# Half of the memory is turned within the half-wide chunk of the first net; turned rows lie in two tiles of weight blocks

## The chip, the cores and the metric

The kernel runs on one core of a Trainium2 chip. The core has a matrix engine (PE, whose weight loads the profile lists apart as PEld), a vector engine (DVE), a scalar engine (ACT), a general engine (POOL) and a queue that issues transfers (SP). Each engine runs its own instructions strictly in the order that the program gives it and waits on semaphores for the others. The metric is the device time of one execution in microseconds (us); before the change it is 1070.46 us, the median of three runs.

## What is computed

The reference is a decoder of two layers over 256 tokens of width 1024 with a memory of 256 rows. In each layer stand a gated net, a mixer, a cross attention into the memory and a second gated net, each with a residual sum and a layer norm. Cut to what matters here:

```python
h = x
for l in range(DEPTH):
    h = layer_norm(ALPHA * h + 0.5 * swiglu(h, ffn1_gate[l], ffn1_up[l], ffn1_down[l]), ...)
    ...                                  # mixer: z = h @ w_in[l], convolution, recurrence, pooling
    h = layer_norm(ALPHA * h + mix, ...)
    h = layer_norm(ALPHA * h + cross_attn(h, mem, ca_q[l], ca_k[l], ca_v[l], ca_o[l]), ...)
    h = layer_norm(ALPHA * h + 0.5 * swiglu(h, ffn2_gate[l], ffn2_up[l], ffn2_down[l]), ...)

def cross_attn(x, mem, wq, wk, wv, wo):
    q, k, v = x @ wq, mem @ wk, mem @ wv     # in four heads
    ...
def swiglu(x, w_gate, w_up, w_down):
    return (jax.nn.silu(x @ w_gate) * (x @ w_up)) @ w_down
```

The hidden width of a net is 2816. The memory `mem` is the same in both layers.

## The kernel before

**Products in two parts.** Every fp32 operand of a large product is split into a high part, rounded for PE's fast format (`whi`, `ah`, the first half of `xT` and `mT`), and a remainder (`wlo`, `al`, the second half). The helper `split` does it with two instructions: a cast on ACT (line 75) and a subtraction on DVE (line 76). A product is then three matmuls: high by high, remainder by high, high by remainder (line 129 issues them all). Weights come by transfers on SP into `raw` tiles of 1024 columns (6 buffers), and the parts into `whi` and `wlo` (8 buffers each), so a cast into `whi` waits until PE has left the tile eight before it.

**The net.** `ffn` runs over chunks of 512 hidden columns; 2816 is five such chunks, 0 to 4, and a last one, chunk 5, of 256 (`last_hidden`). Chunks 2 and 4 (`sevens`) take their products from seven block products instead of eight (`by_seven`), with weight blocks in tiles named `spare0`, `spare1`, `spare2`, `lng`, `lnb` and `raw`. The activations of a chunk are gated on DVE (line 690 for the sevens, line 706 for the last chunk), brought into the order of the second product (`turn`: four transfers and DVE transposes, line 472), and split into `ah` and `al`. The second product of a chunk is run later by `both` into four banks `dn`; the last products, of chunks 4 and 5, stand in `tail`, called from `finish`. For each row tile of 128 tokens and each half of 512 columns, `finish` adds the residual on DVE as soon as that bank is done (line 353), takes the mean and on ACT the squares (line 366), and scales in two steps (lines 374 and 379). PE then transposes the row tile of `h` (line 196) for the next stage: row tile 0 within the tail of row tile 1, row tile 1 within the next stage.

**The memory.** The keys of layer 0 are the stage behind the first net, and they read `mT`, the memory with its width on the partitions and split into two parts. `load_memory` fetches the rows in blocks of 32 into `early_memory` in the middle of the net (POOL's queue, at 100 us), and returns `later`, called `turn_memory` at its use. It turns the blocks of 32 by 32 on DVE (line 220) into `turned`, a tile of tag `up`, of which there is one buffer, and splits `turned` into `mT0` and then `mT1`. `mT1` takes the place of `early_memory`, so its parts are written when all rows have been turned. Before the change this is called once chunk 5 has been recorded, and its instructions on DVE are held behind the last weight remainder recorded until then (`tc.issue_after(lows[-1].ins)`; `lows` lists the subtractions of all splits).

**What sets the order.** Except for a few stretches written by hand, a scheduler orders each engine's instructions when the program is built: by the order in which the code records them, as far as their inputs, free buffers and the edges of `issue_after` allow. An edge holds only instructions of the engine of the instruction that it names. The place where a call stands in the code therefore moves its own instructions and others around them.

## Time and profile before

| what | before |
|---|---|
| median of three runs | 1070.46 us (1069.86 to 1070.7) |
| the profiled execution's own time | 1068.35 us |
| its span, from the first instruction to the last | 1066.6 us |
| granted clock of the matrix engine, mean of the span | 0.998 |
| stretch 129 to 158 us: DVE busy | 23.84 of 29 us |
| stretch 158 to 169 us: DVE busy | 10.89 of 11 us |

The tables of the profile that follow in the prediction are read like this. A timeline row begins with the start in us from the span's start and the time that the row takes, then engine, line, operation, output<-inputs and the form; x3 behind it means three instructions in a row. A bracket gives the idle time of the engine ahead of the row and what ended it. A row of the chain of waits has start, length and what the end of the program was waiting for at that time. A row of waits reads: who waited <- for whom: us in total, times, longest. A PE row's length is from a matmul's start to its end; the next one starts some 0.216 us behind it (512 columns). Tile names are those of the code, without numbers.

### The profile page before, as it was taken

To read this page: it belongs to the slowest core of one execution; us is meant where nothing else is said; L and a number is where in the kernel's file an instruction comes from. 1 tells how busy PE (TensorE), PEld (TensorE's weight loads), DVE (VectorE), ACT (ScalarE), POOL (GpSimd) and SP (SyncE) were. 2 spreads that over 40 slices of the span, in tenths; PEclk is the share of its full clock that TensorE was granted. 3 is DMA by queue.
4 is the path that set the end of the run, shared out by engine and by line. 5 is a ranking of instruction groups with operands and counts; after the bars stand their busy time and mean duration, and the time that the engine had idled before them with its cause. 6 is when DMAs were issued, how large, how long until landed. Compare 5 with 4: busy or idle time off the path is not lost.

```text
span 1066.6 us, 16319 instructions
## 1 busy us (share of the span) xinstructions
PE 1054.6 (99%) x5954; PEld 935.1 (88%) x5954; DVE 915.1 (86%) x1225; ACT 658.8 (62%) x903; POOL 87.2 (8%) x119
## 2 busy tenths in 40 slices
PE   9999999999999999999999999999999999999997
PEld 7888888989899888888888888888998998888886
DVE  6998888989988789897798988689899788899885
ACT  7675765677557557656575757466774655665660
POOL 8001001000000001010001000010000000000000
PEclk9999999999999999999999999999999999999999
DMA  9999983754575589979588978756636675899861
GB/s 364 292 304 297 263 280 116 262 176 159 196 277 172 169 281 238 357 173 293 172 293 221 334 230 258 261 178 217 201 117 222 241 241 165 241 291 304 215 213 40
DMA packets 138897, 248.70 MB, mean 233 GB/s; under 512 B 9472, under 2 KB 48672, under 8 KB 138816
## 3 DMA queue, kind: packets, MB, share of 16 engines
q1 hardware_dynamic: 129024, 228.49, 64.2%
q0 software_dynamic: 9216, 17.98, 9.7%
q10 hardware_dynamic: 576, 1.18, 0.3%
q8 instruction: 47, 0.77, 0.3%
q14 instruction: 34, 0.28, 0.1%
HBM read 232.93 MB, written 1.05 MB: 219 GB/s over the span
## 4 chain that ended last, share of the span: by engine, by line
PE 97%; DVE 2%; DMA 0%; issue 0%; ACT 0%; DVEq 0%; ACTq 0%
PE acc L129 65%; PE dn L129 29%; PE acc L196 1%; DMA h<-in_x_dram 0%; PE dn L990 0%; DVE turned L220 0%; DVE wlo L76 0%; PE dn L1064 0%; DVE mT L76 0%; DVE h L379 0%; PE dn L1063 0%; PE dn L1052 0%; PE acc L1132 0%; DVE h L374 0%; PE dn L1015 0%
## 5 line engine op out<-in xcount | busy, mean ns | idle before, releaser
L76 DVE TENSOR_TENSOR wlo<-raw,whi 128x1024 fp32r<-128x1024 f32 (+1 forms) x444 | 525.9, 1214 | 60.5 <-ACT whi L75 46.1
L75 ACT CAST whi<-raw 128x1024 fp32r<-128x1024 f32 (+1 forms) x444 | 449.9, 1043 | 199.2 <-PE dn L129 63.8
L129 PE MATMUL acc<-whi,xT 128*128 128x512 f32 x992 | 300.7, 379 | 0.0
L129 PEld LDWEIGHTS acc<-whi,xT 128*128 128x128 f32 x992 | 187.5, 189 | 26.5
L129 PE MATMUL acc<-wlo,xT 128*128 128x512 f32 x496 | 188.0, 379 | 0.0
L129 PE MATMUL acc<-xT,whi 128*128 128x512 f32 x576 | 141.0, 381 | 0.2
L129 PE MATMUL dn<-whi,ah 128*128 128x512 f32 x346 | 131.5, 380 | 0.0
L129 PE MATMUL dn<-wlo,ah 128*128 128x512 f32 x346 | 131.1, 379 | 0.0
L129 PE MATMUL dn<-whi,al 128*128 128x512 f32 x346 | 131.1, 379 | 0.0
L129 PEld LDWEIGHTS acc<-xT,whi 128*128 128x128 f32 x576 | 104.1, 190 | 12.5 <-ACT whi L75 0.8
L129 PEld LDWEIGHTS acc<-wlo,xT 128*128 128x128 f32 x496 | 93.8, 189 | 13.2
L129 PE MATMUL dn<-whi,xT 128*128 128x512 f32 x288 | 87.8, 381 | 0.0
L129 PEld LDWEIGHTS acc<-xT,wlo 128*128 128x128 f32 x576 | 75.5, 191 | 3.9
L129 PE MATMUL acc<-xT,wlo 128*128 128x256 f32 x576 | 75.9, 275 | 0.0
L129 PEld LDWEIGHTS dn<-whi,al 128*128 128x128 f32 x346 | 65.4, 189 | 9.3
L129 PEld LDWEIGHTS dn<-wlo,ah 128*128 128x128 f32 x346 | 65.4, 189 | 9.2
L129 PEld LDWEIGHTS dn<-whi,ah 128*128 128x128 f32 x346 | 65.4, 189 | 9.1
L129 PEld LDWEIGHTS dn<-whi,xT 128*128 128x128 f32 x288 | 54.4, 189 | 7.6 <-DVE xT L76 0.2
L129 PE MATMUL dn<-wlo,xT 128*128 128x512 f32 x144 | 54.6, 379 | 0.0
L371 POOL TENSOR_TENSOR rs<-rs,nhalf 128x1 f32<-128x1 f32 x16 | 15.0, 935 | 457.1 <-DVE rs L367 326.4
L129 PE MATMUL acc<-whi,kTh 128*128 128x512 f32 x128 | 48.5, 379 | 0.0
L129 PE MATMUL acc<-wlo,kTh 128*128 128x512 f32 x128 | 48.5, 379 | 0.0
(240 smaller groups left out, 1286.0 us busy)
## 6 DMA issues: line engine op xcount, KB each, us to landing
raw<-in_ffn_up_dram SPq DMA_DIRECT2D x88, 512.0 KB, 5.7
raw<-in_ffn_down_dram SPq DMA_DIRECT2D x88, 512.0 KB, 5.9
raw<-in_ffn_gate_dram SPq DMA_DIRECT2D x84, 512.0 KB, 5.4
raw<-in_w_in_dram SPq DMA_DIRECT2D x48, 512.0 KB, 4.7
dealt<-sg SPq DMA_DIRECT2D x80, 128.0 KB, 5.0
raw<-in_ffn_up_dram POOLq DMA_DIRECT2D x16, 512.0 KB, 7.2
raw<-in_ffn_gate_dram POOLq DMA_DIRECT2D x16, 512.0 KB, 9.2
raw<-in_ca_k_dram SPq DMA_DIRECT2D x16, 512.0 KB, 4.8
```

The costliest lines, as they stand in the source:

```text
L75: nc.scalar.copy(hi, src)
L76: lows.append(nc.vector.tensor_tensor(lo, src, hi.bitcast(F32), op=ALU.subtract))
L129: nc.tensor.matmul(o, w, x, start=start, stop=stop, skip_group_check=more)
L196: nc.tensor.transpose(pt[:, k, :], src[:, (4 * j + k) * P : (4 * j + k + 1) * P], unit)
L371: nc.gpsimd.tensor_tensor(rs, rs, nhalf[:, 0:1], op=ALU.pow)
```

## The change

`later` now takes two numbers, the half of the memory `n` and the pair of blocks `k`, and does a quarter of the work at each call. `turned` lies in the tiles `spare2` (first half) and `spare0` (second half), no longer in the tag `up`, which the last chunk itself uses for its `up` product. `last_hidden` calls it: the two quarters of the first half around the load of the gate weights, one of them held on DVE behind the gating product of chunk 4 (`passed[-1]`), the other behind the last remainder of the gate weights; the two quarters of the second half at its end, as before behind the chunk's own remainders.

```diff
-        def later():
-            for n in range(2):
-                turned = mp.tile([P, NT, CHUNK], F32, tag="up", name="turned", bufs=1)
-                for k in range(2):
-                    nc.vector.transpose(
-                        turned[:, k, :].rearrange("p (k b j) -> p k b j", k=2, j=32),
-                        m[:, 4 * n + 2 * k : 4 * n + 2 * k + 2],
-                    )
+        turned = {}
+
+        def later(n, k):
+            if not k:
+                o = mp.tile([P, DM], F32, tag=("spare2", "spare0")[n], name="turned", bufs=1)
+                turned[n] = o.rearrange("p (k t) -> p k t", t=SEQ)
                 mT.tiles[n] = cst.tile([P, 4, 2, SEQ], F32R, tag=f"mT{n}", name=f"mT{n}")
-                for k in range(2):
-                    d = slice(4 * n + 2 * k, 4 * n + 2 * k + 2)
-                    split(mT[:, d, 0, :], mT[:, d, 1, :], turned[:, k, :].rearrange("p (k t) -> p k t", k=2))
+            o = turned[n][:, k : k + 2]
+            nc.vector.transpose(o.rearrange("p k (b j) -> p k b j", j=32), m[:, 4 * n + k : 4 * n + k + 2])
+            d = slice(4 * n + k, 4 * n + k + 2)
+            split(mT[:, d, 0, :], mT[:, d, 1, :], o)
...
-                    nc.vector.tensor_tensor(s, s, ef, op=ALU.mult)
+                    passed.append(nc.vector.tensor_tensor(s, s, ef, op=ALU.mult))
...
                 for m, o in ((gate, s), (up, r)):
+                    if turn and m is gate:
+                        with tc.issue_after(passed[-1].ins):
+                            turn(0, 0)
                     w = load(m, 0, NK, c0, 2 * P)
+                    if turn and m is gate:
+                        with tc.issue_after(lows[-1].ins):
+                            turn(0, 2)
...
+                if turn:
+                    with tc.issue_after(lows[-1].ins):
+                        turn(1, 0)
+                        turn(1, 2)
                 return ah, al
...
-                    acts.append(hidden(c0) if ncol == CHUNK else last_hidden(c0))
+                    acts.append(hidden(c0) if ncol == CHUNK else last_hidden(c0, turn_memory))
...
-                if c == 5 and early is not None:
-                    with tc.issue_after(lows[-1].ins):
-                        turn_memory()
```

The orders of PE, SP and POOL are the same but for line numbers. Three places of DVE and ACT matter. The first is DVE at the end of chunk 4, from the second difference of its halves (line 643, which was 644) to the last quarter of the first half; `wlo` are weight remainders. Before, and then now, where the rows begin behind the first of these differences and three weight remainders:

```order
L644 TENSOR_TENSOR halves<-acc,halves 128x512
L76 TENSOR_TENSOR wlo<-raw,whi 128x1024 x4
L644 TENSOR_TENSOR halves<-acc,halves 128x512
L76 TENSOR_TENSOR wlo<-raw,whi 128x1024 x2
L644 TENSOR_TENSOR halves<-acc,halves 128x512
L76 TENSOR_TENSOR wlo<-raw,whi 128x1024 x2
L690 TENSOR_TENSOR sg<-sg,halves 128x1024
L76 TENSOR_TENSOR wlo<-raw,whi 128x1024 x4
```

```order
L224 STREAM_TRANSPOSE turned<-early_91 128x512
L76 TENSOR_TENSOR wlo<-raw,whi 128x1024
L643 TENSOR_TENSOR halves<-acc,halves 128x512
L76 TENSOR_TENSOR mT_1344<-turned,mT_1344 128x2x256
L76 TENSOR_TENSOR wlo<-raw,whi 128x1024
L643 TENSOR_TENSOR halves<-acc,halves 128x512
L76 TENSOR_TENSOR wlo<-raw,whi 128x1024 x3
L689 TENSOR_TENSOR sg<-sg,halves 128x1024
L224 STREAM_TRANSPOSE turned<-early_91 128x512
L76 TENSOR_TENSOR wlo<-raw,whi 128x1024 x2
L76 TENSOR_TENSOR mT_1344<-turned,mT_1344 128x2x256
```

Two transposes and two remainders of the memory have come in, the first pair ahead of the fourth split of a row, the second behind the gating product of chunk 4.

The second place is DVE from the gating product of chunk 5 (line 706, now 711) to the residual sums of row tile 0 (line 353, now 352). Before, and then now:

```order
L706 TENSOR_TENSOR sg<-up,sg 128x512
L76 TENSOR_TENSOR al<-sg,ah 128x256 x2
L220 STREAM_TRANSPOSE turned<-early_91 128x512 x2
L76 TENSOR_TENSOR wlo<-raw,whi 128x1024
L76 TENSOR_TENSOR mT_1456<-turned,mT_1456 128x2x256 x2
L76 TENSOR_TENSOR wlo<-raw,whi 128x1024
L220 STREAM_TRANSPOSE turned<-early_91 128x512 x2
L353 TENSOR_SCALAR h_72,st<-h_72,dn 128x512
L76 TENSOR_TENSOR mT_1464<-turned,mT_1464 128x2x256 x2
L353 TENSOR_SCALAR h_72,st<-h_72,dn 128x512
```

```order
L711 TENSOR_TENSOR sg<-up,sg 128x512
L76 TENSOR_TENSOR wlo<-raw,whi 128x1024
L76 TENSOR_TENSOR al<-sg,ah 128x256 x2
L224 STREAM_TRANSPOSE turned<-early_91 128x512 x2
L76 TENSOR_TENSOR wlo<-raw,whi 128x1024
L76 TENSOR_TENSOR mT_1458<-turned,mT_1458 128x2x256 x2
L352 TENSOR_SCALAR h_72,st<-h_72,dn 128x512 x2
```

Two transposes and two remainders are gone from behind the chunk, the two residual sums follow each other, and one weight remainder, of the key weights, has moved ahead of `al`.

The third is ACT at the end of chunk 5, from the casts of the `up` product's weights on. Before, and then now:

```order
L149 COPY up<-acc 128x256 x2
L75 COPY whi<-raw 128x1024
L75 COPY ah<-sg 128x256 x2
L75 COPY whi<-raw 128x1024
L75 COPY mT_1456<-turned 128x2x256
L75 COPY whi<-raw 128x1024
L75 COPY mT_1456<-turned 128x2x256
L75 COPY mT_1464<-turned 128x2x256 x2
```

```order
L149 COPY up<-acc 128x256 x2
L75 COPY whi<-raw 128x1024 x2
L75 COPY ah<-sg 128x256 x2
L75 COPY whi<-raw 128x1024
L75 COPY mT_1458<-turned 128x2x256 x2
```

One more weight cast stands ahead of `ah`; two of the four casts into `mT` have left this place and stand among the weight casts of the first place.

More of the change, by code (lines that the diff above doesn't have):

```diff
@@ L689, in left, with last_hidden @@
                     put(e, o[3], ALU.add, e)
-                    nc.vector.tensor_tensor(s, s, ef, op=ALU.mult)
+                    passed.append(nc.vector.tensor_tensor(s, s, ef, op=ALU.mult))
                     return turn(s)
                 return left
-            def last_hidden(c0):
+            def last_hidden(c0, turn=None):
                 ah, al = act_tiles()
@@ L720, in ffn @@
             sevens = (2, 4)
+            passed, turn_memory = [], None
             bx = []
```

## The prediction

> **What bounds the kernel now.** I read the page first, then the waits of the matmul engine, then the chain of waits around the memory's turning, then the timelines of single engines.

> ```profile
> PE 1054.6 (99%) x5954; PEld 935.1 (88%) x5954; DVE 915.1 (86%) x1225; ACT 658.8 (62%) x903; POOL 87.2 (8%) x119
> ...
> PE 97%; DVE 2%; DMA 0%; issue 0%; ACT 0%; DVEq 0%; ACTq 0%
> ```

> PE works almost without a break and is 97% of the chain. A change on DVE and ACT can matter only where PE stands still. The waits of PE, over the whole span (us in total, times, longest):

> ```profile
> PE acc L196 <- DVE h L379: 1.9, 1, 1.9
> PE dn L493 <- DVE kTh L488: 1.5, 1, 1.5
> PE acc L512 <- DMA h<-in_x_dram: 0.7, 2, 0.5
> ```

> The last two are the start of the program. The first is the one stall behind it, and it happens once: PE is to transpose row tile 0 of `h` behind the first net of layer 0, and the normalized tile is late. PE's timeline there, and at the same place of layer 1, where no memory is turned:

> ```profile
> 170.79 0.38 PE L129 MATMUL dn<-whi,al 128*128 128x512 f32 x1
> 173.10 1.29 PE L196 MATMUL acc<-idn,h 128*128 128x128 f32 x8 [1.93 <-DVE h L379]
> ...
> 174.44 0.38 PE L129 MATMUL dn<-wlo,ah 128*128 128x512 f32 x1
> ```

> ```profile
> 698.32 0.38 PE L129 MATMUL dn<-whi,al 128*128 128x512 f32 x1
> 698.54 1.04 PE L196 MATMUL acc<-idn,h 128*128 128x128 f32 x8
> ...
> 699.63 0.38 PE L129 MATMUL dn<-wlo,ah 128*128 128x512 f32 x1
> ```

> From the last product ahead of the transposes to the second behind them: 174.44 - 170.79 = 3.65 us in layer 0, 699.63 - 698.32 = 1.31 in layer 1. The same instructions cost 2.34 us more where the memory is turned. That is the prize, and all of it.

> Why the tile is late, from the chain:

> ```profile
> 157.49 0.88 DVE al L76 x2
> ...
> 159.05 2.15 DVE turned L220 x2
> ...
> 164.64 2.04 DVE turned L220 x2
> ...
> 167.35 1.29 DVE mT L76 x2
> 168.65 0.62 DVE h L353 x2
> ...
> 172.20 0.76 DVE h L379
> ```

> The four transposes of the memory and their four remainders stand on DVE between the chunk's last split (`al`) and the residual sums of line 353; the second residual sum begins at 168.57 in DVE's timeline, shown below beside layer 1's, which waits for PE alone.

> **The change, part by part.** The work itself stays the same:

> ```profile
> L220 DVE STREAM_TRANSPOSE turned<-early x4: 1132/1144/1184, 159.1 to 165.5; 128x512 f32<-128x512 f32 x4
> L75 ACT CAST mT<-turned x4: 613/616/618, 160.2 to 167.2; 128x512 fp32r<-128x512 f32 x4
> L76 DVE TENSOR_TENSOR mT<-turned,mT x4: 685/714/741, 162.2 to 168.0; 128x512 fp32r<-128x512 f32 x4
> ```

> Four transposes, four casts, four subtractions before and after; nothing on PE, SP or POOL moves. Half of them, 2 x 1.144 + 2 x 0.714 = 3.72 us of DVE and 2 x 0.616 = 1.23 us of ACT, go ahead.

> *Where the first half goes.* One transpose now stands ahead of the third weight split of this stretch, the other behind the gating product of chunk 4. DVE and PE there:

> ```profile
> 129.43 3.82 DVE L76 TENSOR_TENSOR wlo<-raw,whi 128x1024 fp32r<-128x1024 f32 x3 [1.24 <-ACT whi L75]
> ...
> 142.05 1.23 DVE L76 TENSOR_TENSOR wlo<-raw,whi 128x1024 fp32r<-128x1024 f32 x1 [0.57 <-ACT whi L75]
> 143.74 1.23 DVE L76 TENSOR_TENSOR wlo<-raw,whi 128x1024 fp32r<-128x1024 f32 x1 [0.46 <-ACT whi L75]
> 147.29 1.23 DVE L76 TENSOR_TENSOR wlo<-raw,whi 128x1024 fp32r<-128x1024 f32 x1 [2.33 <-PE acc L129]
> ...
> 143.97 1.05 PE L129 MATMUL acc<-xT,wlo 128*128 128x256 f32 x8
> ```

> The third split of the first row ends at 133.25 and PE first reads it at 143.97: 10.7 us in hand against one transpose (1.14) and the cast wait on ACT behind it. DVE's idle time behind the moved rows (0.57 + 0.46 + 2.33 = 3.36 us) nearly holds the 3.72, so I count nothing. If that cover is gone, the lateness reaches the next part, where it has a price.

> *What stands ahead of the chunk's own split now.* With `raw` and `whi` free, the scheduler put the first split of the key weights between the product `sg` and `al`, on ACT and DVE both. Before:

> ```profile
> 156.54 0.38 PE L129 MATMUL dn<-whi,al 128*128 128x512 f32 x1
> 156.58 1.70 ACT L75 CAST ah<-sg 128x256 fp32r<-128x256 f32 x2 [2.18 <-DVE sg L706]
> 157.49 1.67 DVE L76 TENSOR_TENSOR al<-sg,ah 128x256 fp32r<-128x256 f32 x2 [1.00 <-ACT ah L75]
> 160.86 0.19 PEld L129 LDWEIGHTS dn<-whi,al 128*128 128x128 f32 x1
> 161.51 0.19 PEld L129 LDWEIGHTS dn<-whi,al 128*128 128x128 f32 x1
> 160.74 1.04 ACT L75 CAST whi<-raw 128x1024 fp32r<-128x1024 f32 x1
> 161.06 1.24 DVE L76 TENSOR_TENSOR wlo<-raw,whi 128x1024 fp32r<-128x1024 f32 x1
> ```

> The cast is the one at 160.74, the split the one at 161.06. There are 8 `whi` buffers; this cast takes the one that PE leaves with the matmul of 156.54 (the last product of that weight tile), so it can start near 156.54 + 0.38 = 156.9 and ends near 158.0 (1.04). `ah` then starts at 158.0, not 156.58. On DVE the weight split runs from 158.0 to 159.15 (the next instruction starts 1.1 us behind it), and `al` from 159.15 to 160.8. PE loads the first `al` at 160.86, the second at 161.51; ready at about 160.0 and 160.8, where before it was 158.35 and 159.16. The margins shrink from 2.5 and 2.35 us to about 0.85 and 0.7. No stall, but this is the thinnest place of the change.

> *What is left behind the chunk.* Two transposes, one weight split, two remainders. The old timeline has the same five from 159.05 to the split below, 163.36 - 159.05 = 4.31 us; `al` itself held DVE from 157.49 to 159.05, 1.56. So 159.15 + 1.56 + 4.31 = 165.0, and the first residual sum, 0.7 us, ends at 165.7. The second cannot start before PE has finished its bank:

> ```profile
> 163.36 1.28 DVE L76 TENSOR_TENSOR wlo<-raw,whi 128x1024 fp32r<-128x1024 f32 x1
> ...
> 165.61 0.38 PE L129 MATMUL dn<-whi,al 128*128 128x512 f32 x1
> 168.57 0.68 DVE L353 SCALAR_TENSOR_TENSOR h<-h,dn 128x512 f32<-128x512 f32 x1
> 693.56 0.69 DVE L353 SCALAR_TENSOR_TENSOR h<-h,dn 128x512 f32<-128x512 f32 x1 [3.19 <-PE dn L129]
> ```

> That is 165.61 + 0.38 = 166.0, with DVE 0.3 us early; layer 1's sum waits for PE in the same way, and starts 0.04 behind it. So the chain starts 168.57 - 166.03 = 2.54 us sooner, the first half of `h` is done at 172.20 + 0.76 - 2.54 = 170.4, and PE comes to the transposes at 170.79 + 0.22 = 171.0. The pause closes with about 0.6 us over. What is late next: nothing at this place; row tile 1 and the keys follow PE as they do in layer 1.

> *The sum.* Profiled execution 1068.35 us (span 1066.6) - 2.34 = 1066.0. It lies 2.11 below the median of the runs, 1070.46; the same step on the median gives 1068.1. Bounds of the step: 1.93, if only the pause of PE's row closes, and 2.54, the whole advance of the chain. I take 2.34 because layer 1 shows the same instructions without the pause.

> The pause has another size on the weight loads:

> ```profile
> 173.07 0.42 PEld L196 LDWEIGHTS acc<-idn,h 128*128 128x128 f32 x4 [2.30 <-issue]
> 173.73 0.42 PEld L196 LDWEIGHTS acc<-idn,h 128*128 128x128 f32 x4 [0.24 <-PE acc L196]
> ```

> [...]

> **The rivals.** *A smaller pause takes the old one's place.* DVE has 0.3 us over ahead of the second sum and the chain 0.6 behind it. If the row through `al` comes 1.5 us later than worked out (one more weight split of 1.14 and a cast wait), about 0.7 us of stall comes back: 1068.8. For it: both margins are thin and ACT and DVE now wait for each other twice more. Against it: the dates above already hold the split and the cast. At 3 us the gain would be down to nothing.

> *The gain is hidden anyway.* PE runs 2.3 us earlier into the mixer and waits there for transposed rows or weights. Against it: PE's list of waits has no second entry, and layer 1 arrives there without the pause and pays nothing for it. Price: all of it, 1070.4.

> *Slower.* The split through `al` becomes PE's bound. None of the 3.72 us is absorbed ahead of 147.29, since that idle time ends by PE and not by DVE, and all of it comes out on the chunk's chain. `al` is then ready at 160.0 + 3.7 = 163.7 against 160.86: a new stall of 2.9 in the place of 2.34, so 1070.46 + 2.84 - 2.34 = 1071.0. It decides from a lateness of 0.85 + 2.34 = 3.2 us. For it: DVE is 86% busy. Against it: 3.36 us of idle time and more than 10 us in hand at the split that was displaced.

> *The change doesn't do what it says.* The order of DVE shows two of four transposes moved, so I give this no chance of its own.

> **How the numbers follow.** Forecast 0.72, smaller pause 0.15, hidden 0.07, slower 0.06. The predicted time is 1068.1. The forecast's own range: 1070.46 - 2.54 - 0.6 = 1067.3 (0.6 is how far the lowest run lies under the median) to 1070.46 - 1.93 + 0.24 = 1068.8. With most of the smaller pause taken in: 1067.2 to 1069.5. What a measurement of this kernel can tell from no change is about 0.2%, 2.14 us, which is 1068.32: my forecast lies 0.2 us beyond it, so I give three quarters of its 0.72 to faster, 0.54, and one hundredth from the rest for a step larger than worked out: faster 0.55. Slower by over 0.2% begins at 1072.6, beyond the 1071.0 of the slower rival; I let two thirds of that rival's chance run past it, since a chain of late waits between two engines need not stop at the sum of the moved work: 0.04. Same takes the rest, 0.41.

> **What would show it.** In the changed profile: PE's wait for the `h` of line 379 (378 in the changed kernel) is gone from its list; the transposes of `h` follow the product ahead of them within 0.25 us and take 1.04, not 1.29; the second residual sum carries idle time released by PE; the whole-tile splits ahead of chunk 5 run later and PE does not wait for one. The smaller-pause rival would show as a wait of PE for `al`, or again for `h`, under 1 us; the slower one as a PE wait for `al` above 2 us. The prediction is wrong if PE's busy share and its list of waits stay as they are, or if a new wait appears between 129 and 162 us.

## The result, and the profile after

| what | before | after |
|---|---|---|
| median, seven runs of each | 1070.46 us (1068.75 to 1070.83) | 1066.25 us (1065.96 to 1067.75) |
| ratio over all runs, 95% interval | | 0.9966 [0.9954, 0.9978] |
| the profiled execution's own time | 1068.35 us | 1066.03 us |
| its span | 1066.6 us | 1064.3 us |

By the ratio over all runs, which is not the quotient of the medians, the change makes the kernel faster by 0.34% (0.22 to 0.46). Between the medians it is 4.21 us, which is 0.39%, and between the means of the same runs 1070.20 - 1066.55 = 3.6 us. The forecast was 1068.1, with a range that ended at 1067.2: the time lies below it. Yet between the two profiled executions the step is 1068.35 - 1066.03 = 2.32 us, where the sum had 2.34. Both figures are real, and the rest of this document is about the difference between them.

The page of the changed kernel, busy times and the chain by engine, and then PE's complete list of waits:

```profile
PE 1054.4 (99%) x5954; PEld 935.3 (88%) x5954; DVE 915.1 (86%) x1225; ACT 658.3 (62%) x903; POOL 87.4 (8%) x119
...
PE 99%; DMA 0%; DVE 0%; issue 0%; ACTq 0%; DVEq 0%
```

```profile
PE dn L492 <- DVE kTh L487: 1.5, 1, 1.5
PE acc L511 <- DMA h<-in_x_dram: 0.5, 1, 0.5
```

Busy times are the same to 0.5 us. What is gone is the wait for `h`: no entry of PE's list lies behind the start of the program, and DVE's share of the chain has fallen from 2% to nothing. PE's timeline at the transposes of row tile 0 of `h`:

```profile
170.85 0.38 PE L129 MATMUL dn<-whi,al 128*128 128x512 f32 x1
171.07 1.04 PE L196 MATMUL acc<-idn,h 128*128 128x128 f32 x8
171.86 0.46 PE L129 MATMUL dn<-whi,ah 128*128 128x512 f32 x1
172.16 0.38 PE L129 MATMUL dn<-wlo,ah 128*128 128x512 f32 x1
```

From the product ahead of the transposes to the second behind them it is 172.16 - 170.85 = 1.31 us, which is what layer 1 takes, against 3.65 before. DVE and ACT on the way there:

```profile
131.93 1.11 DVE L224 STREAM_TRANSPOSE turned<-early 128x512 f32<-128x512 f32 x1
...
141.54 1.13 DVE L224 STREAM_TRANSPOSE turned<-early 128x512 f32<-128x512 f32 x1
...
147.35 1.23 DVE L76 TENSOR_TENSOR wlo<-raw,whi 128x1024 fp32r<-128x1024 f32 x1 [0.69 <-ACT whi L75]
149.09 1.23 DVE L76 TENSOR_TENSOR wlo<-raw,whi 128x1024 fp32r<-128x1024 f32 x1 [0.52 <-ACT whi L75]
...
157.36 0.69 DVE L711 TENSOR_TENSOR sg<-up,sg 128x512 f32<-128x512 f32 x1
158.11 1.22 DVE L76 TENSOR_TENSOR wlo<-raw,whi 128x1024 fp32r<-128x1024 f32 x1
159.25 1.59 DVE L76 TENSOR_TENSOR al<-sg,ah 128x256 fp32r<-128x256 f32 x2
160.76 2.11 DVE L224 STREAM_TRANSPOSE turned<-early 128x512 f32<-128x512 f32 x2
...
165.10 0.68 DVE L352 SCALAR_TENSOR_TENSOR h<-h,dn 128x512 f32<-128x512 f32 x1
...
166.09 0.69 DVE L352 SCALAR_TENSOR_TENSOR h<-h,dn 128x512 f32<-128x512 f32 x1 [0.30 <-PE dn L129]
```

```profile
157.02 1.05 ACT L75 CAST whi<-raw 128x1024 fp32r<-128x1024 f32 x1 [1.15 <-PE dn L129]
158.14 1.68 ACT L75 CAST ah<-sg 128x256 fp32r<-128x256 f32 x2
```

The idle time of 2.33 us that ended by PE before 147.29 is gone; the split that stood behind it starts at 147.35, so up to there the first half of the memory was paid out of idle time. Behind it DVE does fall back. The split at 149.09 stood behind the sums `sg` of line 150 before (at 150.42) and now stands ahead of the transposes of line 472 (now 471). This move is not among the places listed under the change. DVE waits there for a cast, and the gating product of chunk 5 (line 706, now 711, the row at 157.36 above) starts 1.56 us later than before, where it was:

```profile
155.80 0.68 DVE L706 TENSOR_TENSOR sg<-up,sg 128x512 f32<-128x512 f32 x1
```

It costs nothing, because `ah` cannot start before the weight cast ahead of it has ended, at 157.02 + 1.05 = 158.07, and the late product ends at 157.36 + 0.69 = 158.05. The two meet within 0.02 us. The weight cast starts when PE leaves the `whi` tile, `ah` follows at 158.14, `al` stands on DVE from 159.25 to 160.76, and the second residual sum, at 166.09, has 0.30 us of idle time ended by PE: DVE is early there and PE late, as in layer 1.

### The profile page after: what moved, and what is told of

It reads as the page before. It is cut to its first block, busy times and chain, and to the rows that moved or that the text cites. A ratio compares the mean times of both kernels' runs of the same rounds, so it can differ in the third digit from the quotient of the medians.

```text
span 1064.3 us, 16318 instructions
## 1 busy us (share of the span) xinstructions
PE 1054.4 (99%) x5954; PEld 935.3 (88%) x5954; DVE 915.1 (86%) x1225; ACT 658.3 (62%) x903; POOL 87.4 (8%) x119
## 3 DMA queue, kind: packets, MB, share of 16 engines
HBM read 232.93 MB, written 1.05 MB: 220 GB/s over the span
## 4 chain that ended last, share of the span: by engine, by line
PE 99%; DMA 0%; DVE 0%; issue 0%; ACTq 0%; DVEq 0%
PE acc L129 65%; PE dn L129 31%; PE acc L196 1%; DMA h<-in_x_dram 0%; PE dn L997 0%; PE dn L1071 0%; PE dn L1070 0%; PE dn L1059 0%; PE acc L1139 0%; PE dn L1022 0%; DVE h L378 0%; PE acc L511 0%; DVE h L373 0%; DVE st L358 0%; DVE h L346 0%
## 5 line engine op out<-in xcount | busy, mean ns | idle before, releaser
L76 DVE TENSOR_TENSOR wlo<-raw,whi 128x1024 fp32r<-128x1024 f32 (+1 forms) x444 | 524.7, 1208 | 58.3 <-ACT whi L75 46.2
L75 ACT CAST whi<-raw 128x1024 fp32r<-128x1024 f32 (+1 forms) x444 | 449.5, 1043 | 199.7 <-PE dn L129 66.8
L129 PE MATMUL acc<-whi,xT 128*128 128x512 f32 x992 | 300.7, 379 | 0.0
L129 PEld LDWEIGHTS acc<-whi,xT 128*128 128x128 f32 x992 | 187.5, 189 | 26.5
L129 PE MATMUL acc<-wlo,xT 128*128 128x512 f32 x496 | 188.0, 379 | 0.0
L129 PE MATMUL acc<-xT,whi 128*128 128x512 f32 x576 | 141.0, 381 | 0.2
L129 PE MATMUL dn<-whi,ah 128*128 128x512 f32 x346 | 131.5, 380 | 0.0
L129 PE MATMUL dn<-wlo,ah 128*128 128x512 f32 x346 | 131.1, 379 | 0.0
L129 PE MATMUL dn<-whi,al 128*128 128x512 f32 x346 | 131.1, 379 | 0.0
L129 PEld LDWEIGHTS acc<-xT,whi 128*128 128x128 f32 x576 | 104.1, 190 | 12.5 <-ACT whi L75 0.7
L129 PEld LDWEIGHTS acc<-wlo,xT 128*128 128x128 f32 x496 | 93.8, 189 | 13.2
L129 PE MATMUL dn<-whi,xT 128*128 128x512 f32 x288 | 87.9, 381 | 0.0
L129 PEld LDWEIGHTS acc<-xT,wlo 128*128 128x128 f32 x576 | 75.5, 191 | 3.9
L129 PE MATMUL acc<-xT,wlo 128*128 128x256 f32 x576 | 75.9, 275 | 0.0
L129 PEld LDWEIGHTS dn<-wlo,ah 128*128 128x128 f32 x346 | 65.4, 189 | 9.2
L129 PEld LDWEIGHTS dn<-whi,al 128*128 128x128 f32 x346 | 65.4, 189 | 9.2
L129 PEld LDWEIGHTS dn<-whi,ah 128*128 128x128 f32 x346 | 65.4, 189 | 9.1
L129 PEld LDWEIGHTS dn<-whi,xT 128*128 128x128 f32 x288 | 54.4, 189 | 7.7 <-DVE xT L76 0.3
L129 PE MATMUL dn<-wlo,xT 128*128 128x512 f32 x144 | 54.6, 379 | 0.0
L129 PE MATMUL acc<-whi,kTh 128*128 128x512 f32 x128 | 48.5, 379 | 0.0
L129 PE MATMUL acc<-wlo,kTh 128*128 128x512 f32 x128 | 48.5, 379 | 0.0
```

What stands on the lines that cost most here:

```text
L75: nc.scalar.copy(hi, src)
L76: lows.append(nc.vector.tensor_tensor(lo, src, hi.bitcast(F32), op=ALU.subtract))
L129: nc.tensor.matmul(o, w, x, start=start, stop=stop, skip_group_check=more)
```

## The experiments

The median had moved by 1.9 us more than the profiled execution. Three readings were open. The pause is 2.3 us and the medians differ by more for reasons that have nothing to do with the change, such as where in its spread of times each kernel's seven runs fell. Or the change does something else for the time, by the tiles that `turned` now lies in or by the order of the splits. Or the pause costs more than its length in most executions, and the profiled execution of before was not one of these. The last is called Theory C in the expectations; it took shape with the fifth run, of which below.

The runs above are the first set. The experiments were run in three further sets, each with runs of before of its own; each ratio is against those and is taken over all runs, so it need not be the quotient of the medians.

### Before and after, run again

No edit: before timed again, before profiled a second time, after timed again.

> The kernel before, unchanged. Its profiled execution took 1068.35 us and its runs 1068.75 to 1070.83; the changed kernel's took 1066.03 and 1065.96 to 1067.75. Theory A (the pause varies): the pause of PE ahead of the transposes of h is longer than 1.93 us in executions of 1070 us, about 4 us, and a trace of such an execution shows it there. Theory B (the spread lies elsewhere): a trace of an execution near 1070.4 has the same pause, 1.9 to 2.0, and is longer by 1 to 2 us at another place, at the start of the program above all; then the change is worth 2.3 us in every pair of like executions and part of the measured 4.2 is the draw of executions. Runs here: 1068.3 to 1070.9 by both.

> The kernel before once more, for a second trace. Theory A: where its time is over 1070, the pause at the transposes of h is over 3 us. Theory B: 1.9 to 2.0 us whatever its time.

> The changed kernel, unchanged. Theory A: 3.5 to 4.2 us faster than before again, ratio near 0.9963. Theory B: the ratio of more pairs moves towards 0.9978, that is 2.3 us faster, and runs of both kernels spread over about 2 us.

Measured: before against itself 1070.15 us against 1069.92, ratio 0.9997 [0.9989, 1.0006]. After 1066.68 us (1065.98 to 1066.97), ratio 0.9967 [0.9955, 0.9979]. The gain of the median stands: 3.2 us here, 4.2 in the first set. The times of before are not spread evenly. Of the 22 runs of before in this set six lie from 1068.25 to 1068.51, none between that and 1069.69, and sixteen from 1069.69 to 1071.08. After's six lie from 1065.98 to 1066.97, without such a gap. The fastest differ by 1068.25 - 1065.98 = 2.27 us, the pause again. So before's executions come in two groups, the profile of before (1068.35) was from the lower one, and the median is from the upper. Neither theory of the expectations holds as it stands: a pause of 4 us was not seen, and the gain did not move to 2.3 us.

The second profiled execution of before took 1069.46 us. PE at the pause in its timeline:

```profile
171.90 0.38 PE L129 MATMUL dn<-whi,al 128*128 128x512 f32 x1
174.15 1.29 PE L196 MATMUL acc<-idn,h 128*128 128x128 f32 x8 [1.87 <-DVE h L379]
175.20 0.46 PE L129 MATMUL dn<-whi,ah 128*128 128x512 f32 x1
175.50 0.38 PE L129 MATMUL dn<-wlo,ah 128*128 128x512 f32 x1
```

The pause is nearly as long as in the first profile (1.93), and everything is 174.15 - 173.10 = 1.05 us later. The lateness is there from the first microseconds. PE's first transposes and products of the program, in the first profile of before and in this one:

```profile
5.91 0.48 PE L493 MATMUL dn<-kTh 128*128 128x512 f32 x1
6.59 1.09 PE L512 MATMUL acc<-pdn,h 128*128 128x128 f32 x8 [0.20 <-DMA h<-in_x_dram]
7.44 0.68 PE L129 MATMUL dn<-whi,xT 128*128 128x512 f32 x2
```

```profile
6.60 0.78 PE L493 MATMUL dn<-kTh 128*128 128x512 f32 x1
7.17 1.71 PE L512 MATMUL acc<-pdn,h 128*128 128x128 f32 x8
8.63 0.68 PE L129 MATMUL dn<-whi,xT 128*128 128x512 f32 x2
```

The same matmul takes 0.48 us in one execution and 0.78 in the other, eight transposes 1.09 and 1.71: PE still ran at its lower clock. By the trace's clock records the clock comes up at 5.24 us in the first and at 8.54 in the second; in the other traces whose rise is given in this document, of both kernels, between these two. This spread of about 1 us belongs to no change. It explains a part of the upper group and not all, since 1068.3 + 1.05 ends at 1069.4.

### The tiles alone

After's code with all four quarters turned behind chunk 5, where before turns them, but in the tiles `spare2` and `spare0`. The order on DVE is not quite before's: three transposes now follow each other, and a weight split stands between the two residual sums.

```diff
-                    acts.append(hidden(c0) if ncol == CHUNK else last_hidden(c0, turn_memory))
+                    acts.append(hidden(c0) if ncol == CHUNK else last_hidden(c0))
...
+                if c == 5 and early is not None:
+                    with tc.issue_after(lows[-1].ins):
+                        for n_, k_ in ((0, 0), (0, 2), (1, 0), (1, 2)):
+                            turn_memory(n_, k_)
```

> Both halves turned behind chunk 5 as before, but in the two tiles spare2 and spare0 instead of the one buffer of tag up: the second part of the change alone. My theory (only the place of the first half matters): DVE has the same work ahead of the residual sums, the pause stays at 1.7 to 2.0 us, time within 0.3 us of the kernel before. Rival (the single buffer was the wait, since its second filling waits for the first splits): the pause shrinks by the 1.1 us that the weight split and the refilling took, and the time by 1 us or more.

Measured: 1068.55 us (1068.2 to 1070.94), ratio 0.9994 [0.9985, 1.0002]. PE still waits for `h`:

```profile
PE acc L196 <- DVE h L378: 1.7, 1, 1.7
```

The fastest run, 1068.2, is within 0.1 of before's fastest: in like executions the tiles are worth nothing that can be seen, although the pause is 0.2 us shorter. The median is 1.4 us below before's, more than the 0.3 expected, since only four of the eleven runs lie from 1069.69 up, where sixteen of 22 of before do. Whether the shorter pause makes such executions rarer, or whether this is chance, eleven runs do not show.

### Looking for the upper group

Before unchanged, with a profile, twice.

> The kernel before, for a trace of an execution near 1070.3, of which the runs have most. The traces at 1068.38 and 1069.46 have the same pause of 1.9 us; the second is later by 1.05 from the first 9 us on. Theory B (all of the spread is in the start): an execution of 1070.3 is 2 us later from the first 12 us on, and shows the same pause. Theory C (the pause lets PE's clock fall in some executions): such an execution is about 1 us late behind the start and another 1 us behind the pause at 171 to 173 us, where matmuls stand 0.43 us apart instead of 0.216 for some us.

> As the look before: theory B, any lateness over 1068.3 arises in the first 12 us; theory C, part of it arises at 171 to 178 us.

Measured: 1070.53 and 1068.61 us. The second is the first profile once more, 0.3 us later at the transposes. The first shows the upper group. PE at the pause:

```profile
171.58 0.38 PE L129 MATMUL dn<-whi,al 128*128 128x512 f32 x1
173.88 1.29 PE L196 MATMUL acc<-idn,h 128*128 128x128 f32 x8 [1.92 <-DVE h L379]
174.93 0.56 PE L129 MATMUL dn<-whi,ah 128*128 128x512 f32 x1
175.29 0.63 PE L129 MATMUL dn<-wlo,ah 128*128 128x512 f32 x1
175.71 0.63 PE L129 MATMUL dn<-whi,al 128*128 128x512 f32 x1
176.14 0.63 PE L129 MATMUL dn<-whi,ah 128*128 128x512 f32 x1
...
178.27 0.53 PE L129 MATMUL dn<-whi,al 128*128 128x512 f32 x1
178.64 0.38 PE L129 MATMUL dn<-whi,ah 128*128 128x512 f32 x1
```

The pause is 1.92 us, like every other. But the products behind it take 0.63 us and follow each other every 0.43 instead of 0.38 and 0.216. The same execution by stretches: from and to, length, busy time (and instructions) of PE, PEld, DVE, ACT and POOL, then PE's granted clock, the third number from the right, the share of the transfers and GB/s:

```profile
172.00:175.20 3.20, 1.28 (x9) 1.10 (x10) 3.20 (x7) 2.04 (x3) 1.77 (x2) 0.99 0.00 0
175.20:178.60 3.40, 3.40 (x9) 2.69 (x9) 3.28 (x4) 2.57 (x3) 0.00 (x0) 0.50 0.32 86
178.60:182.00 3.40, 3.40 (x21) 3.08 (x21) 1.10 (x5) 2.62 (x5) 0.23 (x2) 1.00 0.61 222
```

For 3.4 us PE runs at half its clock, and nothing waits for anything: a list of waits does not show this loss. Its price: the transposes begin 173.88 - 173.10 = 0.78 us later than in the first profile, and the spans differ by 1068.7 - 1066.6 = 2.1, so the fall costs 1.3 us. It costs more at first, 1.7: the twelve products behind the transposes take from 174.93 to 179.29, 4.36 us, against 2.67 in the first profile (174.15 to 176.82). Some 0.3 comes back where PE's weight load waits for a cast in the first profile, and in this one, being late, does not:

```profile
188.43 1.38 PEld L129 LDWEIGHTS acc<-xT,whi 128*128 128x128 f32 x7 [0.39 <-ACT whi L75]
```

By the clock records the fall begins at 175.16 us, 167.25 after the clock came up at 7.91, which is 49 times 3.413 us, and the clock stays down for about one such step. In the first profile and in the changed kernel's the clock falls only behind the last matmul, and that too is a whole number of such steps behind the rise: 1058.13 us, 310 of them, in the one, and 1054.72, 309, in the other. A step of 3.413 us, counted from the rise, is called a window from here on. PE was idle for 1.92 us only. What sets the fall off, and whether the transposes count for it, no run here shows; the trace shows how few products stood ahead of it. From the last product ahead of the pause to the first behind the transposes it is about 174.93 - 171.80 = 3.1 us (the last one's start at 171.58 and 0.22 behind it), and the window of 171.75 to 175.16 held some 0.3 us of products at its two ends.

### A larger pause, and a pause without idle time

These two are to tell the clock from the length. Before, with each of the four transposes of the memory issued twice on DVE:

```diff
-                for k in range(2):
+                for k in (0, 1, 0, 1):
                     nc.vector.transpose(
```

> The kernel before with each of the four transposes of the memory issued twice: 4 x 1.04 us more of DVE on the chain into the pause. By the chain the pause grows by 3.6 to 4.1 us, to nearly 6. Theory B: the time grows by just that, 1072 to 1072.5 in the fastest executions. Theory C: behind so long a pause the clock is surely low, matmuls stand 0.43 us apart for about 3 us, and the time grows by another 1 to 1.7 us.

Measured: 1074.84 us (1074.4 to 1075.22), ratio 1.0049 [1.0034, 1.0064]. The list of waits, and the stretches in the trace:

```profile
PE acc L196 <- DVE h L379: 6.0, 1, 6.0
```

```profile
175.30:178.70 3.40, 0.46 (x3) 0.49 (x4) 2.75 (x6) 2.50 (x4) 1.92 (x2) 0.50 0.00 0
178.70:182.20 3.50, 3.50 (x13) 2.96 (x13) 3.09 (x6) 2.12 (x3) 0.00 (x0) 0.51 0.14 26
```

The pause grows by 6.0 - 1.9 = 4.1 us, but the fastest run is 1074.4 - 1068.43 = 6.0 above before's fastest of the same set. Not all of the 1.9 us between the two is the clock. The traced execution spans 1073.2 - 1066.6 = 6.6 us more than the first profile; some 0.9 of it is there from the start, 4.1 is the pause, and about 1.6 is left for the clock. The clock is at half over two windows here, but most of the first holds no product that could be slowed; the products stand in the second. The fall begins at 175.32, again 167.25 behind the clock's rise (8.07). All four runs lie within 0.8 us, and all four show a granted clock of 0.995 over the whole span, where before's show 0.997 to 0.999: with a pause this long there was no lower group in four runs.

Before, with eight products that nobody reads (`kTh` by itself, into a bank of `acc`) on PE ahead of the transposes of `h`:

```diff
+    fills = [8]
+    def filler():
+        if not fills:
+            return
+        x = kTh[:, 0:2, :].rearrange("p k c -> p (k c)")
+        o = acc((P, 512))
+        for _ in range(fills.pop()):
+            nc.tensor.matmul(o, x[:, 0:P], x, start=True, stop=True)
...
-  ... else lambda: transposed(h[0], 0, xTh, xTl, units[0]),
+  ... else lambda: (filler(), transposed(h[0], 0, xTh, xTl, units[0])),
```

> The kernel before, with eight products of no use (a constant tile by itself) issued on PE ahead of the transposes of h, where PE stood still: 8 x 0.216 = 1.73 us of the pause of 1.93 are filled with matmuls, and nothing else moves. Theory C (the gain has two parts, the pause itself and the clock that falls behind it in many executions): the fall goes, no matmul stands 0.43 us apart behind 171 us, all runs lie at 1068.3 to 1069.5 as the start has it, and none of the group from 1069.7 to 1071 is left; about 1 us under the kernel before in the median, and 2.3 us above the changed kernel in the fastest runs. Theory B (all of the spread is in the start): the runs spread as those of the kernel before, median the same within 0.3 us.

PE in its trace:

```profile
171.28 2.03 PE L332 MATMUL acc<-kTh 128*128 128x512 f32 x8
173.33 1.29 PE L196 MATMUL acc<-idn,h 128*128 128x128 f32 x8
174.37 0.46 PE L129 MATMUL dn<-whi,ah 128*128 128x512 f32 x1
174.67 0.38 PE L129 MATMUL dn<-wlo,ah 128*128 128x512 f32 x1
```

The transposes begin no earlier than before, since `h` is no earlier; PE has something to multiply meanwhile. Measured: 1068.42 us (1068.09 to 1069.4) against 1069.75 for before, ratio 0.9988 [0.9979, 0.9997]. In the same set before has thirteen of its 21 runs from 1069.44 to 1071.55; the filled kernel has none above 1069.4, and its fastest, 1068.09, is before's fastest (1068.22) within 0.13. Useless work on the bottleneck engine makes the median 1.3 us faster. That is Theory C: most of these 1.3 us is the clock behind the pause. Not quite all need be, since something else moved against the expectation: the filler also changed the order of ACT and DVE behind the transposes, and the wait of 0.39 us at 188.43 is gone in this trace too. What that is worth was not measured by itself; the fastest runs, which show no effect of the fall, differ by 0.13 us.

The granted clock, which is on record as a mean over the span for every run, points the same way. The traced execution with the fall has 0.997. Over the three further sets 42 of before's 68 runs took 1069.44 us or more: 37 of them have 0.997, five 0.998 and none 0.999. Of the 25 at 1069.09 or less fifteen have 0.999. Of the filled kernel's eleven runs only one has 0.997, and it is the fastest. The sign is not a proof, since the clock also falls behind the last matmul, for a time that varies (3.3 us of the first profile's span, 4.2 of the changed kernel's), and a traced execution of 1068.38 us has 0.997 without a fall at the pause.

### Half the pause

After, with the two transposes of the second half issued twice:

```diff
-            nc.vector.transpose(o..., m[:, 4 * n + k : 4 * n + k + 2])
+            for _ in range(1 + n):
+                nc.vector.transpose(o..., m[:, 4 * n + k : 4 * n + k + 2])
```

> The changed kernel with the two transposes of the second half issued twice: 2 x 1.04 us more of DVE ahead of the residual sums, of which about 0.9 are held by the margins of the changed kernel (0.3 ahead of the second sum, 0.6 behind it). A pause of 1.1 to 1.2 us comes back, with 0.4 more in the transposes. Theory C: the stretch without products is then about 2.4 us, too short for the clock to fall, so the runs lie 1.4 to 1.6 us above the changed kernel's, 1067.4 to 1069.2, in one group with no step behind 171 us. If the clock falls in some of them too, they form a second group above 1069.

Measured: 1068.23 us (1067.32 to 1069.04), ratio 0.9986 [0.9977, 0.9994]. In its list of waits:

```profile
PE acc L196 <- DVE h L379: 1.0, 1, 1.0
```

Its fastest run is 1067.32 - 1066.02 = 1.3 us above the fastest that after's order had in the same set (the kernel of the next section), as long as the pause with its ends: 1.0 in PE's row, and transposes of 1.29 instead of 1.04. All eleven runs lie in one group 1.7 us wide, none of them parted from the others as in before, none has a granted clock of 0.997, and the traced one shows no fall. That trace is a fair test: its clock came up at 8.00 us, so the window 49 steps on is that of 171.84 to 175.25, nearly the one at whose end the clock fell in the execution of 1070.53 us. Here the products are back within it for 1.2 us:

```profile
174.04 0.46 PE L129 MATMUL dn<-whi,ah 128*128 128x512 f32 x1
```

A pause shorter by 0.9 us costs its length, as far as the fastest runs tell; the medians, 1068.23 and 1066.21, stand 2.0 apart, with five runs on one side.

### The second tile, and all of the memory early

After with the second half turned in the tag `up`, where before had it; and after with the second half, too, turned within chunk 5:

```diff
-                o = mp.tile([P, DM], F32, tag=("spare2", "spare0")[n], name="turned", bufs=1)
+                o = mp.tile([P, DM], F32, tag=("spare2", "up")[n], name="turned", bufs=1)
```

```diff
                             turn(0, 2)
+                            turn(1, 0)
+                            turn(1, 2)
...
-                if turn:
-                    with tc.issue_after(lows[-1].ins):
-                        turn(1, 0)
-                        turn(1, 2)
```

> The changed kernel with the second turned half in the tile of tag up again instead of spare0. The order of all engines is the same as the changed kernel's, and up is free where it is used. Expected by my theory: same as the changed kernel, 1066.0 to 1067.8. Rival (the second tile matters): slower by 0.5 us or more, with a wait of DVE ahead of the second half's transposes.

> The changed kernel with the second half of the memory turned within chunk 5 too, behind the gate weights' remainders. My theory of the thin margin: DVE gets 3.7 us more ahead of chunk 5's own split and has about 2.1 us of idle time left there, so al is ready some 1.5 us later than its margin of 0.8 allows, PE waits about 0.5 to 0.9 us for al, and the time is 0.5 to 0.9 us above the changed kernel's, still 1.5 us under the kernel before in like executions. Rival (nothing waits there): no wait of PE for al, time as the changed kernel's within 0.2 us.

Measured: the first 1066.21 us (1066.02 to 1068.09), ratio 0.9967 [0.9955, 0.998], the same as after: the tile `spare0` is worth nothing. The second 1066.91 us (1066.51 to 1067.91), ratio 0.9978 [0.9968, 0.9987], its fastest run 0.55 above after's of the first set; after was not run in its own. PE in its trace:

```profile
161.34 0.38 PE L129 MATMUL dn<-whi,al 128*128 128x512 f32 x1
161.97 0.48 PE L129 MATMUL dn<-whi,ah 128*128 128x512 f32 x1 [0.25 <-ACT ah L75]
162.29 0.38 PE L129 MATMUL dn<-wlo,ah 128*128 128x512 f32 x1
162.93 0.48 PE L129 MATMUL dn<-whi,al 128*128 128x512 f32 x1 [0.26 <-DVE al L76]
163.25 0.38 PE L129 MATMUL dn<-whi,ah 128*128 128x512 f32 x1
```

With another 3.7 us of work ahead of `al` the margin of 0.85 us that the prediction worked out is used up, and PE waits for `ah` and `al`, 0.5 us together in the list of waits. The spacing shows more than the list, as it did at the pause: from 161.34 to 163.25 are four steps, which at 0.216 us would take 0.86 and here take 1.91. This execution took 1067.91 us, against 1066.97 for the second profiled one of the changed kernel, which started about as late. This is the "smaller pause" rival, or rather the slower one in small, made to happen. No kernel that was run is faster than the changed one beyond the spread of the runs.

## Why the prediction was right and wrong

**Where the work went: right, at one place by luck.** The first half early costs PE nothing, as forecast. But the prediction put its cost on the chunk's own chain at nothing too, for the idle time that it saw ahead of 147.29, and there the gating product of chunk 5 came 1.56 us later. That this was free is because the cast ahead of `ah` holds the chain to 158.07 anyway; the prediction's dates had that cast in them and not the lateness beside it. The cast ahead of `ah` was put near 156.9 and starts at 157.02; `ah` at 158.0, measured 158.14; `al` from 159.15 to 160.8, measured 159.25 to 160.76; the first residual sum ended by 165.7, measured 165.78; the second at 166.0 waiting for PE, measured 166.09 with 0.30 us of idle time; PE at the transposes at 171.0, measured 171.07.

**The pause: right.** 2.34 us by layer 1's example; 2.32 between the two profiled executions, 2.27 and 2.3 between fastest runs, 1.31 us where layer 1 has 1.31. That the two profiled executions agree so well is luck in part: their clocks came up at 5.24 and 5.42 us, and neither shows a fall of the clock at the transposes. Of the two other sizes, the 1.93 us of PE's row was too small and the 2.54 of the weight loads (2.30 + 0.24) too large.

**The rivals: none came.** No wait took the old one's place, nothing hid the gain, and `al` was in time. Moving the other half as well showed that the margin there was as thin as stated.

**The failing step: "That is the prize, and all of it", and with it "the same step on the median gives 1068.1".** The step was measured in one execution and put on the median of others. The prediction wrote down that the profiled execution lies 2.11 us below the median, and drew nothing from it but the same step further up. That number was the sign: the profile was of an execution of the lower group. In the upper group the same pause is followed by 3.4 us of half clock, 1.3 us more, and the start is slower, by 0.78 us in the one that was traced: 0.78 + 1.3 = 2.1. The change takes away the half clock and not the slower start. So the pause was worth 2.3 us in some executions and 2.3 + 1.3 = 3.6 in others, and the median before is one of the others: 1070.46 - 3.6 = 1066.9 would have been the forecast, where 1066.25 and, in the later sets, 1066.68 and 1066.21 were measured. What is left of the first set's 4.21, some 0.6 us, is within what the start moves; against the later sets' runs of before the medians gain 3.2 and 3.5. The means agree, by an estimate from these figures: with sixteen of 22 runs in the upper group the gain should be 2.3 + 1.3 x 16/22 = 3.2 us, and the means of that set differ by 3.2; with thirteen of 21 in the last set it should be 3.1, and they differ by 3.1.

The range failed for the same reason: it allowed 0.6 us for how runs lie about their median and held nothing for a second effect of the pause.

**Still open.** What sets off the fall of the clock. In the execution of 1069.46 us the window that ended 49 steps behind the rise, at 8.54 + 167.25 = 175.79, held some 0.6 us of products behind 175.20, and there was no fall; in the one of 1070.53 about 0.3, and there was; that the amount of products decides is not shown by two executions. Nor is it known what sets the time of the rise at the start. Of four profiles of before taken later one shows the fall, while 42 of 68 runs lie in the upper group; that runs without a trace fall as the traced one did is shown by their group's end in the filled kernel and by the granted clocks, not by traces of them. Nor is the fall the whole of the spread. Single runs of the changed kernel and of its order with `up` took 1067.75 and 1068.09 us, 1.8 and 2.1 above the fastest, where the starts that were traced explain about 1; five of before's upper runs have a granted clock of 0.998, above that of the traced fall. What delays these is not shown.

## What to carry to other kernels

Where the profiled execution lies off the median by about as much as the expected gain, the difference is a term of the sum: profile the same kernel several times until both groups of its times have been seen, and only then size the edit. Here a pause of the matrix engine cost more than its length: in the execution where the clock fell, 1.92 us with 1.05 us of transposes behind them were followed by 3.4 us at half the clock, 1.3 us of time, which shows in no list of waits but in the spacing of the products, 0.43 us instead of 0.216. Eight products that nobody reads, put where PE stood still, lowered the median by 1.3 us and moved the fastest run by 0.13.
